# A hybrid layer on one core: instructions are recorded first and issued by a list scheduler written in the kernel

## Chip, core and metric

One core of a Trainium2 chip runs the whole kernel. The metric is device time in microseconds from the first to the last instruction of one execution. The times of the kernel before come from three runs. One further execution was taken with the hardware profiler, and all rows below are of that one.

## The reference

One layer of a trunk with five parallel head groups on 2048 tokens of width 1024, in float32. Cut to what matters:

```python
def hybrid_layer(x, mem, ...):
    h = rms_norm(x, norm_g)
    proj = h @ w_in                                  # one projection, 1024 -> 4652 columns
    pa, pb, pc, pd, pm = split_cols(proj, GROUP_COLS)
    ya = spatial_gating(...)                         # A: gMLP, chunks of 128 tokens
    yb = forgetting_attention(...)                   # B: FoX, causal attention with decay
    yc = mlstm(...)                                  # C: matrix memory, chunks of 128
    yd = rwkv7_time_mix(token_shift(pd, rwkv_mu), ...)   # D: delta rule, a state carried over all tokens
    ym = memory_attention(...)                       # M: attention to 256 memory tokens
    branches = [(ya, a_z), (yb, b_z), (yc, c_z), (yd, d_z), (ym, m_z)]
    mixed = jnp.concatenate([y * jax.nn.silu(z) for y, z in branches], axis=-1)
    return x + mixed @ w_out                         # 1280 -> 1024
```

Each group has 4 heads of width 64.

## The kernel before

**Stages.** Phase 1 normalises x, projects the columns of RWKV-7 (blocks `Dk`, `narrow`, `Dr`, `Dv`, `Dz`) for four quarters of 512 tokens, and runs RWKV-7 (`front` and `back`) beside it. Phase 2 goes over the quarters again for the columns of the mLSTM and of FoX, with the mLSTM beside it, and the RWKV-7 that is left. Phase 3 projects the columns of the gMLP and of the memory attention and runs FoX beside it. Then comes the output projection (line 878), with the memory attention beside its beginning. In the profiled execution phase 1 runs from 0 to about 245 us, phase 2 begins to mix with it there and goes on to about 960 us, phase 3 ends at about 1470 us, the memory attention at about 1602 us.

**Projections.** Weights come from DRAM into `wraw` (line 210, on SP's DMA queue), are split into two float32r parts `wt` by ACT (line 221) and DVE (line 224), and are multiplied with the two parts `ht` of the normalised tokens (ACT line 328, DVE line 329). The matmuls into the PSUM banks `pj` are lines 266, 277, 288, 300 and 314. They use the full 128*128 array. The norm of the tokens comes from `rstd`, which loads x a second time into `xt` (line 362, also on SP).

**Work beside them.** Most other matmuls have operands of 64 rows or 64 columns and take part of the array. In a profile's row the numbers before the tile's shape say which: 128*64 is all rows and half of the columns. In the attentions, line 1080 and line 1083 make scores in `p`, ACT takes the exponential to `pe` (line 1085), POOL adds these up (lines 1097, 1099), and line 1106 multiplies them with `v` into `acc`, in 64 columns of the array. RWKV-7's chain from chunk to chunk is line 1462 (`sv,gt`), a copy to `xc`, line 1471 (`xc,x`), a copy to `qv`, lines 1479 and 1481, and two DVE instructions that make the next `sv`. `front` computes 1/|k| of each token and head in `rn`: `rsqrt` (lines 151 to 155) does this by Newton's steps in eleven small DVE instructions, each of which reads what the one ahead of it wrote; line 1307 stands ahead of them, and PE's line 1319 waits for the last. In the attentions, `maxima` ends in line 1019, which makes `mm`, and PE's line 1067 waits for that.

**What sets the order.** `body` is Python that emits instructions. While it emits a projection it calls `tick()` after every few matmuls:

```python
    def tick():
        step_w()
        evac.tick()
        for l in lanes.values():
            l.tick()
```

`step_w` goes on with the loading of the next weights, `evac` holds what reads finished projections, and each lane is a queue of generators that goes on by its rate (`RATES`: gate 0.4, mlstm 0.8, front 1.0, back 1.33, fox 1.815 stages for each tick). So each engine's order is first the order of the program, with small pieces of the side work sprinkled between parts of the projections by fixed rates. The framework (Tile) then puts in the waits, assigns the buffers, and moves instructions by a cost model of its own.

Of the kernel before, what the change touches and what calls it, by code (L numbers as in the profile page):

```python
# [18 lines left out]
P = 128  # L19
# [16 lines left out]
# 256-column blocks of the input projection, by the first column of each  # L36
# [8 lines left out]
# narrow columns: (first column, width, first row of the transposed block)  # L45
NARROW = [(3340, 16, 0), (2564, 4, 16), (2568, 4, 20), (1536, 4, 24), (3868, 16, 32)]

# columns of the packed per-partition parameters
# [15 lines left out]
class Lane:  # L64
    """a queue of work that is emitted a stage at a time, between the parts of the projections"""
# [19 lines left out]
class Crowd:  # L85
    """short pieces of work that go on side by side, a stage at a time; a stage that has read a projection for the last
    time gives FREE"""
# [9 lines left out]
    def add(self, g, kind=None, most=2):  # L97
        """kind: what takes the same buffers, of which there are so many"""
        while sum(k == kind for _, k in self.all) >= most and kind:
            self.tick()  # L100
        if self.step(g):
            self.all.append((g, kind))
# [8 lines left out]
    def then(self, g):  # L111
        """g, behind all that is under way now"""
# [5 lines left out]

@with_exitstack
def body(ctx: ExitStack, tc, x, xT, mem, memT, wp, wkv, wout, pv, wa, sguT, sgub, out, dbg=None):  # L120
    nc = tc.nc
# [16 lines left out]
    ident = cp.tile([P, P], F32, name="ident")  # L138
    make_identity(nc, ident)
# [7 lines left out]
    def rsqrt(t):  # L147
        """in place, of up to 16 positive columns: half of the exponent, negated, then Newton's steps to the last bit"""
# [8 lines left out]
    # parameters that stand behind a tanh, a doubled SiLU or a doubled GELU  # L157
# [47 lines left out]
    def load_w(parts, src, ncol=256):  # L205
        """hi and lo parts of a block of 256 columns, 2 row blocks to a tile"""
# [42 lines left out]
    def W(n):  # L249
        """the weights of this block; those of the next one are sent for"""  # L250
# [9 lines left out]
    def proj_T(wt, m, hts):  # L260
        """[128 columns, 512 tokens] of the projection"""
# [10 lines left out]
    def proj_narrow(wt, hts):  # L272
        """64 columns: the products of their hi parts above those of the lo parts"""
# [8 lines left out]
    def proj_T2(wt, hts, then=None):  # L282
        """both halves of a block at once: for the last use of the row blocks"""
# [10 lines left out]
    def proj_tok2(wt, hts, then=None, ntile=4):  # L294
        """all tokens at once"""
# [11 lines left out]
    def proj_tok(wt, hts, i):  # L307
        """[128 tokens, 256 columns] of the projection, twice: tokens i * 128 on and the next 128"""
# [11 lines left out]
    def split_h(hts, src_of, g, N):  # L320
        """hi and lo parts of (normalised x) * g, one tile for each of the 8 row blocks"""
# [16 lines left out]
    def send(*a):  # L338
        """the next row blocks are sent for"""
        nxt[0] = []  # L340
        nxt[1] = split_h(nxt[0], *a)
        next(nxt[1])
        return nxt[1]
# [6 lines left out]
    def rstd(pool, tags, src, ntile):  # L350
        """1/rms of each token, tokens on partitions; tags: of the buffers for half of the columns of 128 tokens"""
# [20 lines left out]
    def rstd_rows(pool, tags, rb, src, ntile):  # L372
        """1/rms of each token, as a row over all partitions"""
# [4 lines left out]
    def over(ss, rb, ntile):  # L378
        """from tokens on partitions to a row over all partitions"""
# [5 lines left out]
    def gate(pt, o, then=lambda: None, free=FREE):  # L385
        """twice the SiLU"""
# [6 lines left out]
    def head_norm(pt, n, eps, pool=None):  # L393
        """1/rms over the 64 columns of each head; n columns on 128 tokens"""
# [13 lines left out]
    def qk_post(y, scale, d):  # L408
        """normalised over each head, scaled, transposed: to d"""
# [30 lines left out]
    def tok_cols(wt, hts, i, d):  # L440
        """tokens on partitions, to DRAM"""
# [10 lines left out]
    with ExitStack() as c1:  # L452
# [12 lines left out]
        def first(hts):  # L465
            """the first tokens: the norm is put to what comes out, so that the products need not wait for it"""
# [58 lines left out]
        for q in range(NQ):  # L525
# [8 lines left out]
            def shifted(pt, j, then):  # L534
                """token shift of a block of 128 columns"""
# [72 lines left out]
        evac.drain()  # L608

# [1142 lines left out]
```

## Time and profile before

| | us |
|---|---|
| three runs | 1751.72, 1748.99, 1744.91 |
| median | 1748.99 |
| span of the profiled execution | 1753.3 |
| PE busy | 1654.2 (94%), 11306 matmuls |
| DVE busy | 1197.5 (68%), 2990 instructions |
| ACT busy | 880.9 (50%), 1895 instructions |
| POOL busy | 302.8 (17%), 356 instructions |
| mean granted TensorE clock | 0.977 |

The profiled execution's own time is known by its span alone, which is 4.3 us over the median of the three runs. Busy times come from the page of the profile. Matmuls are pipelined and their ends are modelled, so a busy PE is not a PE at its peak: the time from the start of one group of matmuls to the start of the next tells more than the busy share.

### The profile page before, as it was taken

Reading aid. Unit: us, or ns where it says so; the run is one execution under the profiler, and the core shown is the slowest. Engines: PE = TensorE matmul, PEld = TensorE weight load, DVE = VectorE, ACT = ScalarE, POOL = GpSimd, SP = SyncE. Lnnn points to the kernel's source line nnn. Section 1 sums busy time; section 2 is a strip of 40 time slices with the busy share of each in tenths; the row PEclk is TensorE's granted clock in tenths of the full one; section 3 lists DMA queues with packets and bytes.
Section 4 is the critical chain, followed back from the end, with each engine's and each line's share of the span. In section 5 each row is a group of like instructions: output and inputs, shape, how many; then the busy total and the mean of one; then the engine's idle time right before and its main releaser. Section 6 shows DMA issues by size and latency. Waiting matters only on the chain.

```text
span 1753.3 us, 31654 instructions
## 1 busy us (share of the span) xinstructions
PE 1654.2 (94%) x11306; PEld 1282.0 (73%) x11306; DVE 1197.5 (68%) x2990; ACT 880.9 (50%) x1895; POOL 302.8 (17%) x356
## 2 busy tenths in 40 slices
PE   8889999899999999999999899998999998899999
PEld 6667777787978888787888666756655665577887
DVE  7688684775978579587766986878576777642220
ACT  5566654544464545446455765565555657531110
POOL 5020000010101001010000244354444142000000
PEclk9999999899999999999999999999999999899999
DMA  6878554443544354344435554434324335754431
GB/s 207 259 236 245 179 173 101 137 118 94 144 130 122 104 149 124 85 123 129 119 88 167 148 152 112 109 95 121 85 78 111 106 77 162 184 142 122 129 125 59
DMA packets 200151, 234.36 MB, mean 134 GB/s; under 512 B 75016, under 2 KB 107336, under 8 KB 199992
## 3 DMA queue, kind: packets, MB, share of 16 engines
q1 hardware_dynamic: 185144, 218.69, 43.6%
q10 hardware_dynamic: 14848, 13.64, 2.6%
q8 instruction: 89, 1.46, 0.4%
q14 instruction: 70, 0.57, 0.1%
HBM read 180.44 MB, written 51.81 MB: 132 GB/s over the span
## 4 chain that ended last, share of the span: by engine, by line
PE 58%; DVE 18%; DMA 14%; ACT 6%; issue 4%; SPq 1%; POOL 0%; ACTq 0%; DVEq 0%; POOLq 0%
PE pj L266 12%; PE pj L878 12%; PE pj L314 11%; DMA wraw<-in_wp 4%; PE pj L288 3%; PE acc L1106 3%; DMA xr<-hbd 3%; DVE wt L224 2%; PE wk L1025 2%; DMA ao<-dn 2%; PE p L1080 2%; PE p L1083 1%; PE pj L300 1%; DMA xr<-in_xT 1%; DVE rq L153 1%
## 5 line engine op out<-in xcount | busy, mean ns | idle before, releaser
L266 PE MATMUL pj<-ht,wt 128*128 128x512 f32 x1632 | 427.6, 404 | 6.0 <-ACT ht L328 4.2
L266 PEld LDWEIGHTS pj<-ht,wt 128*128 128x128 f32 x1632 | 298.3, 190 | 83.8 <-issue 9.8
L314 PE MATMUL pj<-wt,ht 128*128 128x256 f32 x2400 | 337.3, 292 | 6.9 <-ACT ht L328 2.4
L314 PEld LDWEIGHTS pj<-wt,ht 128*128 128x128 f32 x2400 | 308.1, 195 | 24.6 <-issue 5.8
L224 DVE TENSOR_TENSOR wt<-wraw,wt 128x512 fp32r<-128x512 f32 (+1 forms) x312 | 220.3, 709 | 94.0 <-ACT wt L221 92.5
L221 ACT CAST wt<-wraw 128x512 fp32r<-128x512 f32 (+1 forms) x312 | 184.7, 600 | 148.8 <-DMA wraw<-in_wp 103.1
L878 PE MATMUL pj<-wo,mt 128*128 128x512 f32 x960 | 232.7, 399 | 2.5 <-ACT wo L829 2.3
L878 PEld LDWEIGHTS pj<-wo,mt 128*128 128x128 f32 x960 | 180.3, 190 | 53.7 <-issue 6.9
L1099 POOL TENSOR_TENSOR es<-es,pe 128x512 f32<-128x512 f32 (+3 forms) x128 | 155.2, 1212 | 107.9 <-ACT pe L1085 99.2
L288 PE MATMUL pj<-ht,wt 128*128 128x512 f32 x480 | 135.5, 421 | 13.3 <-ACT wt L221 12.4
L1085 ACT ACTIVATE pe<-p 128x512 f32<-128x512 f32 x192 | 100.7, 541 | 67.9 <-PE p L1083 65.4
L1039 DVE TENSOR_REDUCE mx<-wk 128x1 f32<-128x512 f32 (+3 forms) x192 | 112.5, 615 | 16.6 <-PE wk L1025 11.2
L288 PEld LDWEIGHTS pj<-ht,wt 128*128 128x128 f32 x480 | 91.2, 199 | 38.1 <-ACT wt L221 12.8
L1106 PE MATMUL acc<-pe,v 128*64 128x512 f32 (+3 forms) x384 | 106.9, 580 | 5.9 <-DVE at L1139 5.1
L1097 POOL TENSOR_TENSOR es<-pe 128x512 f32<-128x512 f32 (+1 forms) x32 | 43.3, 1353 | 249.3 <-ACT pe L1085 207.1
L329 DVE SCALAR_TENSOR_TENSOR ht<-xr,pvt,ht 128x512 fp32r<-128x512 f32 (+1 forms) x88 | 68.6, 786 | 24.8 <-ACT ht L328 24.1
L858 ACT CAST mt<-mr 128x256 fp32r<-128x256 f32 x80 | 31.9, 406 | 102.7 <-DVE xr L882 45.9
L1080 PE MATMUL p<-qa,kb 128*128 128x512 f32 x192 | 76.9, 400 | 6.7 <-ACT pe L1085 6.7
L328 ACT ACTIVATE ht<-xr,pvt 128x512 fp32r<-128x512 f32 (+1 forms) x88 | 61.0, 701 | 42.5 <-DMA xr<-hbd 26.7
L882 DVE TENSOR_TENSOR xr<-pj,xr 128x512 f32<-128x512 f32 x32 | 22.0, 688 | 85.6 <-PE pj L878 85.5
L1025 PEld LDWEIGHTS wk<-ka,qb 66*128 66x128 f32 x224 | 40.4, 191 | 49.5 <-issue 17.7
L1025 PE MATMUL wk<-ka,qb 66*128 66x512 f32 (+3 forms) x224 | 72.5, 378 | 4.2 <-DVE mx L1039 1.4
(332 smaller groups left out, 2471.5 us busy)
## 6 DMA issues: line engine op xcount, KB each, us to landing
wraw<-in_wp SPq DMA_DIRECT2D x288, 256.0 KB
xr<-hbd SPq DMA_DIRECT2D x56, 256.0 KB
mr<-mix SPq DMA_DIRECT2D x80, 128.0 KB
xr<-in_x SPq DMA_DIRECT2D x32, 256.0 KB
out<-xr ACTq DMA_DIRECT2D x32, 256.0 KB
xt<-in_x SPq DMA_DIRECT2D x24, 256.0 KB
xr<-in_xT SPq DMA_DIRECT2D x24, 256.0 KB
hbd<-xr SPq DMA_DIRECT2D x24, 256.0 KB
```

The costliest lines, as they stand in the source:

```text
L221: A.copy(wt[:, :, 0, :ncol], raw[:, :, :ncol])
L224: V.tensor_tensor(lo, raw[:, :, :ncol], wt[:, :, 0, :ncol].bitcast(F32), op=ALU.subtract)
L266: T.matmul(pt, wt[k // 2][:, k % 2, a, m * P:(m + 1) * P], hts[k][:, b, :], start=n == 0, stop=n == 3 * KT - 1)
L288: T.matmul(pts[m], wt[k // 2][:, k % 2, a, m * P:(m + 1) * P], hts[k][:, b, :], start=k + n == 0, stop=k == KT - 1 and n == 2)
L314: T.matmul(pt[:, ii * 256:ii * 256 + 256], hts[k][:, a, (i + ii) * P:(i + ii + 1) * P], wt[k // 2][:, k % 2, b, :], start=n == 0, stop=n = ...
L878: T.matmul(po, mts[i // 2, k][:, a, i % 2 * P:(i % 2 + 1) * P], wo[e * NK + k][:, b], start=n == 0, stop=n == 3 * NK - 1)
L1025: T.matmul(p1, self.qb[0:66, i * P:(i + 1) * P], self.k[kk][0][0:66, :w], start=True, stop=True, skip_group_check=diag)
L1039: V.tensor_reduce(*late.pop(), axis=AX.X, op=ALU.max)
L1080: T.matmul(p2[:, f:], kb[:, ks], self.qa[:, f:], start=True, stop=False)
L1085: A.activation(e[:, f:], p2[:, f:], AF.Exp)
L1099: G.tensor_tensor(self.sum[:, f:], self.sum[:, f:], e[:, f:], op=ALU.add)
L1106: self.att.nc.tensor.matmul(self.acc[64 * i:64 * i + 64, f:], self.v[:, kt], e[:, f:], start=kt < 2, stop=True, skip_group_check=True)
```

## The change

`body` now runs with `nc = rec = Recorder(tc.nc, tc)` and with the framework's own re-ordering switched off. A call such as `V.tensor_tensor(...)` no longer issues anything. It is kept as an `Op` with the operations that it depends on (found from the boxes of the tiles that it reads and writes) and a price in nanoseconds. At five places `rec.flush()` issues all that was recorded since the last one: at the end of phase 1, between phases 2 and 3 (where the pools change), at the end of phase 3, behind the last unit of the attentions, and at the end of the program. No instruction moves across a flush. Rates, stages, tiles, buffers and the instructions themselves stay as they were, and comments are taken out. The diff, cut to its core:

```diff
+    def price(self, o):
+        if o.fn == "dma_start":
...
+            o.cost, o.lag, o.key = 400.0, 1900.0, packets * each / 16
+        if e == "tensor":
...
+            q = [32 if x <= 32 else 64 if x <= 64 else 128 for x in (rows, cols)]
+            if lhs.dtype == F32R:
+                c = max(n / 2.4 + 14, 60.0)
...
+            o.cost, o.mode, o.lag = c, tuple(q), 200.0
...
+        if e == "vector":
+            if o.fn in ("tensor_tensor", "scalar_tensor_tensor", "tensor_reduce"):
+                o.cost = 150 + 1.06 * n
...
+    SWITCH = {True: 95.0, False: 100.0}
+
+    def flush(self):
...
+        while left:
+            best = None
+            for e, lst in cand.items():
+                if not lst:
+                    continue
+                c = self.pick(e, lst, first)
+                if c and (best is None or c[:2] < best[:2]):
+                    best = c
+            start, _, o = best
+            cand[o.eng].remove(o)
+            self.place(o, start, live)
...
+        for o in order:
+            getattr(getattr(self.nc, o.eng), o.fn)(*o.a, **o.k)
...
+    def after(self, p, o):
+        if p.eng == o.eng and p.fn != "dma_start":
+            return 0.0
+        return p.done + self.SEM
...
+    def pick(self, e, lst, first):
...
+            s = max(clk, o.ready, r + self.SEM if r else 0.0)
+            n = o.n
+            if e == "tensor" and self.mode not in (None, FULL):
+                if o.mode != FULL and o.mode == self.mode and s <= clk + 60:
+                    n -= 1 << 30
+                elif o.mode != FULL and s <= clk + 60:
+                    n -= 1 << 29
+            c = (s, n, o)
...
-    nc = tc.nc
+    nc = rec = Recorder(tc.nc, tc)
+    ctx.enter_context(tc.manual_schedule())
...
+        rec.flush()
```

In words: of all operations whose predecessors are placed, the one that can start first by these prices is placed next. Of those that can start together, the one that comes first in the program goes first. PE has one more rule: while the array is in a part shape, a matmul of the same shape that can start within 60 ns goes ahead of all others, and then one of any part shape. An operation on the same engine as its predecessor costs no lag (`after`). Buffers of a tag are given out in the order of the program (`room`).

The instructions are the same in number on each engine; their order differs. Three places show how. (All rows of the kernel after carry line 350, where `flush` issues them, so tiles tell what they are.)

PE, FoX beside the projections of phase 3, where `p` are score banks with the program's running numbers. Before:

```order
L314 MATMUL pj<-wt,ht 128x256 x12
L1080 MATMUL p_16855<-qa,kb 128x512
L1083 MATMUL p_16855<-qb,ka 128x512
L1106 MATMUL acc<-pe,v 64x512 x2
L1080 MATMUL p_16866<-qa,kb 128x512
L1083 MATMUL p_16866<-qb,ka 128x512
L314 MATMUL pj<-wt,ht 128x256 x12
L1080 MATMUL p_16888<-qa,kb 128x512
L1083 MATMUL p_16888<-qb,ka 128x512
L1106 MATMUL acc<-pe,v 64x512 x2
L1080 MATMUL p_16896<-qa,kb 128x512
```

After:

```order
L350 MATMUL p_12971<-qa,kb 128x512
L350 MATMUL p_12971<-qb,ka 128x512
L350 MATMUL p_12973<-qa,kb 128x512
L350 MATMUL p_12973<-qb,ka 128x512
L350 MATMUL wk<-ka,qb 128x256 x2
L350 MATMUL pj<-wt,ht 128x256 x8
L350 MATMUL acc<-pe,v 64x512 x8
L350 MATMUL pj<-wt,ht 128x256 x4
L350 MATMUL p_12978<-qa,kb 128x512
```

Four to eight `acc<-pe,v` matmuls now stand in one row where two stood, with fewer returns to the projections `pj` between. Over the whole program, PE comes back from a part shape to the full array 268 times, where it was 365 (phase 1 44 and 44, phase 2 169 and now 141, phase 3 134 and now 74, output projection 17 and now 9). Changes from one part shape to another are 121, where they were 106.

DVE, the inverse norm `rn` of RWKV-7's `front`, from its first to its last instruction (before, only the first half of it). Before:

```order
L1307 TENSOR_SCALAR rn<-wk 128x8
L1404 TENSOR_TENSOR xs<-xs,xtmp 128x3x23
L151 TENSOR_SCALAR rq<-rn 128x8
L1309 SCALAR_TENSOR_TENSOR ag<-th,gi 128x512
L1403 TENSOR_TENSOR xtmp<-xs,at 128x3x22
L153 TENSOR_TENSOR rq<-rq 128x8
L1311 TENSOR_SCALAR th<-th,hp_70 128x256
L1404 TENSOR_TENSOR xs<-xs,xtmp 128x3x22
L154 SCALAR_TENSOR_TENSOR rq<-rq,rn 128x8
L1311 TENSOR_SCALAR th<-th,hp_70 128x256
L1403 TENSOR_TENSOR xtmp<-xs,at 128x3x21
L155 SCALAR_TENSOR_TENSOR rq<-rq 128x8
```

After:

```order
L350 TENSOR_SCALAR rn<-wk 128x8
L350 TENSOR_SCALAR rq<-rn 128x8
L350 TENSOR_TENSOR rq<-rq 128x8
L350 SCALAR_TENSOR_TENSOR rq<-rq,rn 128x8
L350 SCALAR_TENSOR_TENSOR rq<-rq 128x8
L350 TENSOR_TENSOR rq<-rq 128x8
L350 SCALAR_TENSOR_TENSOR rq<-rq,rn 128x8
L350 SCALAR_TENSOR_TENSOR rq<-rq 128x8
L350 TENSOR_TENSOR rq<-rq 128x8
L350 SCALAR_TENSOR_TENSOR rq<-rq,rn 128x8
L350 SCALAR_TENSOR_TENSOR rn<-rq 128x8
L350 SCALAR_TENSOR_TENSOR ag<-th,gi 128x512
```

The eleven instructions stand one behind the other now. Before, 15 to 28 rows lay between the first and the last in the eight blocks; nine of them are its own. Over the program, 1428 of DVE's instructions read what the one directly ahead of them wrote; before, 653 did.

SP's DMA queue in phase 1, where `xt` are the second loads of x for the norm and `wraw` the weights (of `Dz`, here). Before:

```order
L582 DMA gated<-sh 12x512
L362 DMA xt<-in_x 128x512 x3
L584 DMA smd<-sh 16x2x512
L362 DMA xt<-in_x 128x512 x3
L584 DMA smd<-sh 16x2x512
L362 DMA xt<-in_x 128x512 x2
L553 DMA d_r<-sh 128x512
L210 DMA wraw<-in_wp 128x512 x3
```

After:

```order
L350 DMA xt<-in_x 128x512
L350 DMA hbd<-x_137 128x512
L350 DMA wraw<-in_wp 128x512
L350 DMA xr<-in_xT 128x512
L350 DMA gated<-sh 12x512
L350 DMA smd<-sh 16x2x512 x2
L350 DMA hbd<-x_145 128x512
L350 DMA wraw<-in_wp 128x512
L350 DMA d_r<-sh 128x512
L350 DMA xt<-in_x 128x512
L350 DMA wraw<-in_wp 128x512
L350 DMA xt<-in_x 128x512
```

Before, all eight loads of `xt` stand ahead of the first weights of `Dz`; now the weights stand between the loads of `xt`, the first of them behind one.

At the flush between phases 1 and 2 no projection stands between three steps of RWKV-7's chain on PE: `rw<-sv,gt`, `rw<-xc`, `rw<-qv,gt` and the next `rw<-sv,gt` follow each other directly.

## Rows read from the trace of the kernel before

**Rows 1.** Span of the core and its mean granted TensorE clock.

```profile
core 0: 1753.3 us, clock 0.977
```

**Rows 2.** Windows: length, busy PE, PEld, DVE, ACT, POOL, clock, DMA share, GB/s.

```profile
360.00:960.00 600.00, 584.89 (x5435) 497.00 (x5436) 438.11 (x1359) 297.92 (x662) 40.97 (x89) 0.99 0.42 121
960.00:1470.00 510.00, 478.95 (x2639) 330.17 (x2637) 386.20 (x740) 302.06 (x597) 196.62 (x161) 0.97 0.42 112
...
1602.00:1753.30 151.30, 147.56 (x641) 119.26 (x633) 33.26 (x65) 16.34 (x41) 0.00 (x0) 1.00 0.34 107
sum 1753.30, PE 1654.17 PEld 1282.02 DVE 1197.49 ACT 880.86 POOL 302.84; mean PE 275.70 PEld 213.67 DVE 199.58 ACT 146.81 POOL 50.47
```

**Rows 3.** The page's chain that ended last: share of the span by engine.

```profile
PE 58%; DVE 18%; DMA 14%; ACT 6%; issue 4%; SPq 1%; POOL 0%; ACTq 0%; DVEq 0%; POOLq 0%
```

**Rows 4.** The chain, 250 to 350 us: start, length, undisturbed projections with their count.

```profile
260.99 10.88 PE pj L288 x48
271.87 5.99 PE pj L314 x50
```

**Rows 5.** PE's timeline, 286 to 289 us, RWKV-7: start, length, line, tiles, array, count.

```profile
286.02 0.45 PE L1462 MATMUL rw<-sv,gt 128*64 128x64 f32 x8
286.40 0.75 PE L314 MATMUL pj<-wt,ht 128*128 128x256 f32 x4
287.08 0.48 PE L1471 MATMUL rw<-xc,x 64*64 64x64 f32 x8
...
288.15 0.69 PE L1479 MATMUL rw<-qv,gt 128*64 128x64 f32 x16
288.77 0.33 PE L1481 MATMUL rw<-sv,rk 64*64 64x64 f32 x2
```

**Rows 6.** PE's timeline, 1444 to 1446 us, FoX beside a projection.

```profile
1444.19 1.66 PE L266 MATMUL pj<-ht,wt 128*128 128x512 f32 x6
1445.78 0.65 PE L1106 MATMUL acc<-pe,v 128*64 128x256 f32 x4
```

**Rows 7.** PE's waits by releaser: us in total, times, longest us.

```profile
PE pj L288 <- ACT wt L221: 12.4, 2, 7.5
PE wk L1067 <- DVE mm L1019: 11.5, 8, 3.1
PE wk L1319 <- DVE rn L155: 8.6, 6, 3.0
...
PE acc L1106 <- DVE at L1139: 5.1, 3, 2.5
...
PE wk L1146 <- DVE mx L1039: 4.1, 2, 3.7
```

**Rows 8.** DVE's timeline, 237 to 248 us: first and last instruction of one `rn`.

```profile
237.79 0.16 DVE L1307 TENSOR_SCALAR rn<-wk 128x8 f32<-128x8 f32 x1
...
247.78 0.15 DVE L155 SCALAR_TENSOR_TENSOR rn<-rq 128x8 f32<-128x8 f32 x1
```

**Rows 9.** DVE's timeline, 21 to 24 us: neighbours, the first two independent, the last dependent.

```profile
21.77 0.16 DVE L151 TENSOR_SCALAR rq<-ss 128x4 int32<-128x4 int32 x1
21.84 0.28 DVE L224 TENSOR_TENSOR wt<-wraw,wt 128x128 fp32r<-128x128 f32 x1
...
23.39 0.15 DVE L154 SCALAR_TENSOR_TENSOR rq<-rq,ss 128x4 f32<-128x4 f32 x1
23.58 0.16 DVE L155 SCALAR_TENSOR_TENSOR rq<-rq 128x4 f32<-128x4 f32 x1
```

**Rows 10.** SP's timeline, 41 to 52 us: first `xt` loads, and the weights behind all.

```profile
41.28 1.60 SPq L362 DMA_DIRECT2D xt<-in_x  x3
...
51.56 1.45 SPq L210 DMA_DIRECT2D wraw<-in_wp  x3
```

**Rows 11.** Windows around PE's gap in phase 1; columns as in rows 2.

```profile
53.20:58.20 5.00, 0.05 (x2) 0.01 (x1) 1.18 (x8) 1.64 (x7) 0.00 (x0) 0.79 0.84 266
56.10:62.90 6.80, 4.71 (x15) 3.80 (x16) 4.67 (x16) 3.09 (x5) 0.00 (x0) 0.50 0.76 249
```

More of the change, by code (lines that the diff above doesn't have):

```diff
@@ L138, in body @@
     ident = cp.tile([P, P], F32, name="ident")
-    make_identity(nc, ident)
+    make_identity(tc.nc, ident)
     pvt = cp.tile([P, NPV], F32, name="pvt")
@@ L772, in body @@
                     l.step()
+            rec.flush()
             csp.close()
@@ L815, in body @@
     evac.drain()
+    rec.flush()
     cw.close()
@@ L839, in body @@
         fox.step()
+    rec.flush()
     att.c5.close()
@@ L884, in body @@
                 nc.scalar.dma_start(out[r, es], xr)
+    rec.flush()
     att.close()
```

238 lines of the change are left out of this document (added).

## The prediction

> **What bounds the kernel now.** I began with the span and the clock [rows 1], then the windows by stage [rows 2], then the chain that ended last [rows 3]. PE is busy for 1654.2 of 1753.3 us and idle for 99.1 (the difference in the sum row). DVE, the next, has 438 of 600 us in phase 2 and 386 of 510 in phase 3. PE holds 58% of the chain and DVE 18%. So PE sets the time, and two kinds of loss can be looked for on it: time in which it is busy but slower than it could be, and time in which it waits.
>
> *Busy but slow.* Undisturbed projections set the scale: 48 matmuls of 512 columns in 10.88 us, 0.2267 each, and 50 of 256 columns in 5.99 us, 0.1198 each [rows 4]. Beside RWKV-7 four of the latter take 0.68 us from their start to the start of what follows (286.40 to 287.08), where 4 x 0.1198 = 0.48 would do: 0.20 us go when PE returns from a part of the array to the whole [rows 5]. On the way in, eight `sv,gt` matmuls take 0.38 us (286.02 to 286.40), while sixteen like them take 0.62 (288.15 to 288.77). Eight more cost 0.24, so the first eight carry 0.14 of their own. A round trip costs 0.20 + 0.14 = 0.34 us. FoX's products show the same: six projections take 1.59 us (1444.19 to 1445.78) where 6 x 0.2267 = 1.36 would do, 0.23 on the way out [rows 6]. At 365 trips this is about 124 us of PE's busy time.
>
> *Waiting.* The longest waits are for weights (ACT `wt`, 12.4 us) and for ends of DVE's chains: `mm` 11.5, `rn` 8.6, `at` 5.1, `mx` 4.1, together 29.3 [rows 7]. The largest single gap is in phase 1: PE has 0.05 us of work in 53.2 to 58.2, and the clock granted behind it, from 56.1 to 62.9, is 0.50 of full speed, 1.2 GHz instead of 2.4 [rows 11]. The mean clock of 0.977 [rows 1] says what such stretches take over the whole: 0.023 x 1753 = 40 us, if PE had work in all of them.
>
> **The change part by part.** Its instructions are the same, so it can only remove losses or add some.
>
> *A, round trips.* The order after has 97 returns to the whole array fewer, 60 of them in phase 3 and 28 in phase 2, and 15 more changes from one part shape to another. 97 x 0.34 = 33.0 us less. A change between part shapes has no row of its own; I put it at the entry's 0.14, so 15 x 0.14 = 2.1 us more. A gives -31. All of it lies on PE, which has least slack: in 360 to 960 us it is busy for 584.9 of 600 [rows 2]. The other bound is 0, where the time saved on PE comes back as waiting.
>
> *B, weights ahead of the second loads of x.* All eight `xt` loads stand in SP's queue ahead of the weights of `Dz`, from 41.28 to 51.56 us [rows 10], and the gap of 4.95 us follows. After, only one stands ahead. The `xt` loads that weights now pass are late instead; what waits for them is the norm of the first tokens, on ACT and DVE, whose product comes behind the matmuls. I count the gap, -5.0, and leave the 3.4 us that the half clock takes of the next 6.8 (half of them) for the bound: 0 to -8.4. The DMA engines are busy for 0.76 to 0.84 of that time [rows 11], so transfers are not made faster by being re-ordered.
>
> *C, PE's other waits.* Of the 99.1 us idle, 5.0 are in B and 3.7 in the last stage (151.30 less 147.56), which has no side work to move: some 90 are left. The `rn` chain now lasts from 237.79 to 247.78, 10.0 us, with up to 19 other instructions in it [rows 8]. With eleven neighbours at 0.195 us each (23.39 to 23.58) [rows 9] it takes 2.1, so its 8.6 us of waits go. Between the first and the last of `mm` the order has 2.2 rows where it had 3.7 on the mean: 1.5 rows less of at most 0.7 us, for 8 waits, -7. Together -16. Of the rest, 90 - 16 = 74, the scheduler's order takes the shorter ones by time and not by fixed rates. Nothing in the trace prices that; between none and half (-37) I take a fifth, -15, since most of them end with an engine that itself has little slack. With a third of the idle time gone (31 of 90) a third of the 40 us of low clock could go, -13; short waits carry less of it, so I take -10. C gives -41, bounds 0 and -80.
>
> *D, flushes.* Nothing moves across a flush. At the one between phases 1 and 2, three steps of RWKV-7's chain now stand with no projection between. A step takes 1.06 us (286.02 to 287.08), 0.38 of it matmuls [rows 5], so 0.68 lie open: 3 x 0.68 = 2. Two such flushes, 4 us; the others fall where only one kind of work is left. Bounds 0 and +10 (five flushes).
>
> *E, dependent neighbours on DVE.* An instruction that reads what the one ahead of it wrote starts 0.195 us after it; an independent one starts 0.07 after it (21.77 to 21.84) [rows 9]. So each new pair costs DVE 0.12 us, and there are 1428 - 653 = 775 more: 93 us on DVE, from 1197 to about 1290. DVE has idle time to hide this (162 us in 360 to 960, 124 in 960 to 1470 [rows 2]). Where the cover is gone the cost is one for one. I take DVE's share of the chain, 18% [rows 3]: +17, bounds 0 and +93.
>
> [...]
>
> *Sum.* -31 - 5 - 41 + 4 + 17 = -56. Against the profiled execution's span this is 1753.3 - 56 = 1697. That span lies 4.3 us over the median of the three runs, 1749.0, so the time to forecast is 1749 - 56 = **1693 us**. With half of A and of C it would be 1729; with E at nothing, 1676.
>
> **The rivals.** *1, more of the waits go.* If half of the 90 us of waits and half of the 40 us of clock go, with A at -33, B at -8.4, D at +4 and E at 0, the sum is -45 - 20 - 33 - 8 + 4 = -102: 1647 us. For it: every engine but PE has about a third of its time free or more, and the order is made with all engines in view. Against it: the scheduler's prices are fixed figures, and its lag on the same engine is zero, which rows 9 contradict.
>
> *2, what feeds PE sets the pace.* PE's savings come back as waits, since the projections cannot go on before ACT and DVE have read the banks and delivered `ht` and `wt`. A is 0, C halves to -20: -5 - 20 + 4 + 17 = -4, 1745 us, no change. For it: 42% of the chain is not PE [rows 3], and DVE has only 24% free in phase 3. Against it: in phase 2 PE idles for 15 us of 600 only, and nothing that feeds it is near 100%.
>
> The Trainium skill, "TensorEngine Tiling (Array Packing)", section "PSUM Bottleneck", says that using parts of the array speeds up TensorE but not the reading of PSUM, which may then become the bottleneck. Here fewer trips squeeze the same reads into less time; by that rule rival 2 is the outcome, while the 68% of DVE and 50% of ACT speak for room.
>
> *3, slower: DVE becomes what PE waits for.* DVE takes its queue in order, so a chain of eleven dependent instructions, 2.1 us, now holds up every weight split and bank copy behind it, where before these stood in its gaps. If that keeps all of C's waits in place and 62 of the 93 us (two thirds) reach PE, the sum is -31 - 5 + 4 + 62 = +30: 1779 us. It decides from the point where, with C at 0, 41 of the 93 us (44%) land on PE: -31 - 5 + 4 + 41 = +9. For it: 29.3 us of waits already end with DVE [rows 7]. Against it: DVE's 286 us of idle time in phases 2 and 3, and the chains end sooner for those who wait for them.
>
> That the change does not do what it says is ruled out by the order: the counts in A are the kernel's own.
>
> **How the numbers follow.** Chances: forecast 0.50 (its own range 1670 to 1720), rival 1 0.22, rival 2 0.13, rival 3 0.15. About 0.5% (8.7 us) is what a measurement of this kernel can tell from no change. Forecast and rival 1 are faster, with a part of rival 2: 0.75. Same is most of rival 2, 0.11. Slower is rival 3 with its nearer part, 0.14. The range goes from 1635 (a little beyond rival 1) to 1755 (rival 2, and the point at which rival 3 begins), which leaves out most of rival 3 and the ends of rival 1.
>
> **What would show it.** A: `acc` rows of six to eight in phase 3, and PE's time from the start of a product to the next projection unchanged, 0.20 to 0.23 over the steady rate. B: no PE gap around 53 us, weights of `Dz` on the way before 45 us. C: PE's waits for `rn` near 0 and for `mm` under 5 us, idle time near 65 us, mean clock over 0.98. D: three short gaps where phase 1 ends. E: DVE busy or bound in short gaps for about 90 us more, with the eleven `rn` instructions 0.19 to 0.20 apart. The forecast is wrong if PE's idle time stays near 99 us or grows (rivals 2 and 3; in 3 most of its waits end with DVE), or if DVE's pairs cost PE more than 31 us. It is also wrong if a trip does not cost 0.34 us when eight matmuls stand in a row instead of two.

## The result: 1.3% slower, and where PE's time went

The kernel after takes 1774.05 us (median of 4 runs, 1769.09 to 1778.78), the kernel before 1748.8 (4 runs). The ratio is 1.0129, with a 95% interval from 1.0095 to 1.0164: some 23 us slower, where the forecast was 56 us faster. Since the kernel before was run again beside each group of experiments, what follows compares ratios to it; 0.01 is 17.5 us.

The page of the kernel after: span, busy times, and the chain by engine; then span and clock.

```profile
span 1769.2 us, 31645 instructions
...
PE 1638.6 (93%) x11306; PEld 1293.1 (73%) x11306; DVE 1263.1 (71%) x2990; ACT 882.3 (50%) x1895; POOL 305.0 (17%) x356
...
PE 47%; DVE 22%; DMA 19%; issue 4%; ACT 4%; SPq 1%; ACTq 1%; POOL 0%; DVEq 0%; POOLq 0%
```

```profile
core 0: 1769.2 us, clock 0.971
```

PE is busy for 15.6 us less than before (1654.2) and idle for 1769.2 - 1638.6 = 130.6 us, 31.5 more than the 99.1 of [rows 2]. DVE is busy for 65.6 us more. In the chain PE falls from 58% to 47%, DVE goes from 18 to 22 and DMA from 14 to 19 [rows 3]. The mean clock falls from 0.977 [rows 1] to 0.971: 0.029 x 1769 = 51 us at most, where it was 40.

To compare stages, the windows are cut in each kernel where the projections of phases 1, 2 and 3 end. Columns as in [rows 2]. Before:

```profile
0.00:271.90 271.90, 245.11 (x1379) 189.44 (x1380) 203.37 (x507) 158.68 (x373) 39.85 (x74) 0.97 0.69 211
271.90:952.30 680.40, 656.15 (x6013) 555.21 (x6011) 496.17 (x1526) 341.52 (x758) 51.20 (x110) 0.98 0.42 120
952.30:1477.50 525.20, 491.78 (x2726) 340.65 (x2725) 393.11 (x755) 309.33 (x612) 197.73 (x162) 0.97 0.43 115
1477.50:1753.30 275.80, 261.14 (x1193) 196.72 (x1191) 104.84 (x203) 71.32 (x156) 14.07 (x11) 0.98 0.44 127
```

After:

```profile
0.00:293.50 293.50, 257.74 (x1555) 195.32 (x1557) 214.75 (x511) 160.25 (x383) 35.64 (x73) 0.95 0.61 191
293.50:987.40 693.90, 648.26 (x5837) 556.76 (x5837) 533.30 (x1520) 335.41 (x735) 52.59 (x108) 0.97 0.42 118
987.40:1486.40 499.00, 469.65 (x2725) 344.23 (x2724) 408.52 (x749) 311.27 (x612) 203.92 (x165) 0.99 0.41 115
1486.40:1769.20 282.80, 262.99 (x1192) 196.79 (x1192) 106.55 (x210) 75.39 (x167) 12.88 (x10) 0.96 0.47 137
```

Phase 3 is 26.2 us shorter (525.2 to 499.0): 60 of the 97 saved returns are there, and its clock is higher as well (0.99 where it was 0.97). Phase 1 is 21.6 longer, of which a part is RWKV-7's work done earlier (1555 matmuls where there were 1379). Phase 2 has 176 matmuls and 7.9 us of PE's work less, and is 13.5 us longer all the same, so PE is idle for 45.6 us there instead of 24.3. DVE has 37 us more to do in it. The last stage is 7.0 longer. Together these make the 15.9 us between the two spans.

PE's waits in the kernel after (us in total, times, longest):

```profile
PE pj L350 <- DVE wt L350: 17.7, 17, 3.9
PE pj L350 <- ACT wt L350: 16.5, 7, 7.6
PE p L350 <- ACT pe L350: 12.1, 10, 4.7
PE pj L350 <- DVE ht L350: 8.4, 7, 2.9
...
PE wk L350 <- DVE mm L350: 3.9, 9, 1.1
...
PE wk L350 <- DVE rn L350: 0.9, 2, 0.6
```

The waits that the prediction named have shrunk: `rn` from 8.6 to 0.9, `mm` from 11.5 to 3.9 [rows 7]. Others have grown, for weights above all. Projections now wait 17.7 us for DVE's half of them and 16.5 for ACT's, which was 13.5 before. For DVE's half, the two largest waits of the kernel before were these:

```profile
PE pj L277 <- DVE wt L224: 1.7, 1, 1.7
...
PE pj L314 <- DVE wt L224: 0.7, 2, 0.3
```

One such place, in rows of the kernel after. ACT's timeline first: it has copied a block of weights by 680.51 (679.89 + 0.62), and the split that DVE has to make of it may begin then.

```profile
679.89 0.62 ACT L350 CAST wt<-wraw 128x512 fp32r<-128x512 f32 x1
```

DVE's timeline, from just ahead of that:

```profile
679.83 0.17 DVE L350 TENSOR_SCALAR rq<-rs 128x8 int32<-128x8 int32 x1
680.04 0.17 DVE L350 TENSOR_TENSOR rq<-rq 128x8 f32<-128x8 f32 x1
...
682.64 0.17 DVE L350 TENSOR_SCALAR rq<-rs 128x8 int32<-128x8 int32 x1
...
687.40 0.69 DVE L350 TENSOR_TENSOR wt<-wraw,wt 128x512 fp32r<-128x512 f32 x1
```

And PE's:

```profile
688.14 2.08 PE L350 MATMUL pj<-wt,ht 128*128 128x256 f32 x8 [3.93 <-DVE wt L350]
```

An `rsqrt` that has just begun, a second one behind it, and other work, of RWKV-7 above all, stand ahead of the split. An `rsqrt` has ten instructions; with the one that feeds it that makes the chain of eleven of the prediction, at 0.20 us from start to start, each reading what the one ahead of it wrote. The split of the weights waits for 6.9 us in DVE's queue (680.51 to 687.40), and PE for 3.93.

A second kind of place, beside the output weights `wo`. ACT's timeline:

```profile
1500.80 0.62 ACT L350 CAST wo<-wr 128x512 fp32r<-128x512 f32 x1 [1.89 <-issue]
...
1503.43 0.62 ACT L350 CAST wo<-wr 128x512 fp32r<-128x512 f32 x1 [1.20 <-DMA wr<-in_wout]
1504.43 0.62 ACT L350 CAST qa<-kr 128x512 fp32r<-128x512 f32 x1 [0.38 <-DMA kr<-qk_Mq]
1504.96 0.59 ACT L350 ACTIVATE pe<-p 128x512 f32<-128x512 f32 x1
```

PE's at the same time:

```profile
1500.94 0.63 PE L350 MATMUL p<-qa,kb 128*128 128x512 f32 x1
1505.60 0.80 PE L350 MATMUL p<-qa,kb 128*128 128x512 f32 x1 [4.03 <-ACT pe L350]
```

The scores that `pe` reads are there by about 1501.6 (1500.94 + 0.63). But ACT stands before copies whose loads have not landed (it waits for them for 1.20 and 0.38 us more), with the exponential queued behind them, and PE waits for 4.03 us. In the scheduler's account a load takes 0.4 us to issue and lands 1.9 us plus its transfer later, about 3 us for 256 KB. Of the 17 weight loads of 256 KB in the chain of the kernel after, 15 take 3.6 to 6.9 us and two take 2.7 and 2.9. The chain has the loads that were waited for, so the mean of all may be lower. Two of them:

```profile
41.01 4.04 DMA wraw<-in_wp
...
435.85 6.94 DMA wraw<-in_wp
```

### The profile page after: what moved, and what is told of

Its sections match the earlier page's. It is cut to its first block, busy times and chain, and to the rows that moved or that the text cites. A ratio compares the mean times of both kernels' runs of the same rounds, so it can differ in the third digit from the quotient of the medians.

```text
span 1769.2 us, 31645 instructions
## 1 busy us (share of the span) xinstructions
PE 1638.6 (93%) x11306; PEld 1293.1 (73%) x11306; DVE 1263.1 (71%) x2990; ACT 882.3 (50%) x1895; POOL 305.0 (17%) x356
## 3 DMA queue, kind: packets, MB, share of 16 engines
q8 instruction: 89, 1.46, 0.4%
## 4 chain that ended last, share of the span: by engine, by line
PE 47%; DVE 22%; DMA 19%; issue 4%; ACT 4%; SPq 1%; ACTq 1%; POOL 0%; DVEq 0%; POOLq 0%
PE pj L350 32%; PE rw L350 6%; PE wk L350 5%; DMA wraw<-in_wp 4%; DVE wt L350 3%; DVE rq L350 3%; PE p L350 2%; PE acc L350 2%; DMA xr<-in_xT 2%; DVE xtmp L350 2%; DMA xr<-hbd 2%; DVE xs L350 2%; DMA mr<-mix 1%; DVE mx L350 1%; SPq L350 1%
## 5 line engine op out<-in xcount | busy, mean ns | idle before, releaser
L350 PE MATMUL pj<-ht,wt 128*128 128x512 f32 x2176 | 576.4, 409 | 32.6 <-ACT wt L350 9.7
L350 PEld LDWEIGHTS pj<-ht,wt 128*128 128x128 f32 x2176 | 405.1, 193 | 140.6 <-DVE wt L350 15.4
L350 PE MATMUL pj<-wt,ht 128*128 128x256 f32 x2784 | 396.3, 293 | 19.3 <-DVE wt L350 9.3
L350 PEld LDWEIGHTS pj<-wt,ht 128*128 128x128 f32 x2784 | 359.5, 195 | 40.3 <-DVE wt L350 10.9
L350 DVE TENSOR_TENSOR wt<-wraw,wt 128x512 fp32r<-128x512 f32 (+1 forms) x312 | 232.3, 750 | 79.0 <-ACT wt L350 78.4
L350 POOL TENSOR_TENSOR es<-es,pe 128x512 f32<-128x512 f32 (+3 forms) x128 | 159.8, 1249 | 97.0 <-ACT pe L350 91.0
L350 PE MATMUL acc<-pe,v 128*64 128x512 f32 (+3 forms) x384 | 100.1, 569 | 8.2 <-ACT pe L350 5.6
L350 ACT ACTIVATE ht<-xr,pvt 128x512 fp32r<-128x512 f32 (+1 forms) x88 | 60.8, 701 | 55.3 <-DMA xr<-hbd 31.5
L350 PE MATMUL p<-qb,ka 68*128 68x512 f32 x192 | 74.7, 392 | 0.0
L350 DVE TENSOR_TENSOR xtmp<-xs,at 128x60 f32<-128x60 f32 (+24 forms) x248 | 61.2, 247 | 6.5 <-DMA at<-ad 2.6
L350 PEld LDWEIGHTS acc<-pe,v 128*64 128x64 f32 x384 | 28.0, 137 | 50.8 <-issue 24.7
```

The costliest lines, as they stand in the source:

```text
L350: getattr(getattr(self.nc, o.eng), o.fn)(*o.a, **o.k)
```

## The experiments

Two theories stood after this. **D**: DVE's dependent neighbours cost it some 90 us (step E of the prediction) and hold up what PE needs. **M**: loads are priced too short, so engines stand blocked before work whose data is on its way.

The expectations count dependent neighbours by the operations themselves: 534 before, 1220 after. The counts of 653 and 1428 in the change go by the tiles' names without buffer numbers, and so take in neighbours that work on different buffers.

**Each price alone.** The first edit charges a DVE instruction by the rows and lets one that reads its neighbour's output start only 114 ns later, so that other work is put between. The second lets a DMA land later.

```diff
-            return 0.0
+            if p.eng == "vector" and p.outs & o.ins:
+                return p.done + 84.0        # done is the end plus 30
+            return 0.0
...
+            o.cost -= 80                    # e == "vector"
```

> The kernel after with one price changed: a DVE instruction is priced 80 ns less, and one that reads what the instruction ahead of it on DVE wrote may start 114 ns after that one's end at the earliest (rows 9 give both). The scheduler then puts other work between: by the order, neighbours that depend on each other fall from 1220 rows to 612 (before: 534), and PE's returns to the whole array stay at 265 (after: 268). Theory D, dependent neighbours on DVE cost the time: DVE's busy time falls from 1263 to about 1205, PE's waits for the weights (wt, 34 us of waits by DVE and ACT) about halve, PE's idle time falls from 131 to about 100 us, and the time from 1774 to about 1735 (1720 to 1750). Theory M, loads are priced too short, so engines stand blocked behind them: 1765 to 1778, PE's waits as they are.

```diff
-            o.cost, o.lag, o.key = 400.0, 1900.0, packets * each / 16
+            o.cost, o.lag, o.key = 400.0, 3200.0, packets * each / 16
```

> The kernel after with one price changed: a DMA lands 3.2 us after its issue plus its transfer, not 1.9 (in the chain of after, loads of 256 KB take 4.0 to 4.9 us, where the old price gives about 3). Neighbours on DVE that depend on each other stay (1224 rows), PE's returns are 284 (after: 268). Theory M, loads priced too short: ACT waits less for wraw (148 us of idle time ended by it in after, 103 before), PE's idle time falls by 15 to 25 us, the time to 1745 to 1758. Theory D: 1768 to 1782, with 16 more returns worth 5 us more.

Measured: 1756.07 us for the first, ratio 1.0042 [1.0015, 1.0069]; 1752.98 for the second, ratio 1.0000 [0.9973, 1.0026]. Both gain on the after's 1.0129. The second is as M expected. The first lies between the two expectations: DVE's busy time and PE's waits for weights (`wt`, 34.2 us after, 13.5 here) fall as D said, and the time gains less than half of what D said. The page's row of the first, with DVE back near the 1197.5 of before:

```profile
PE 1630.0 (93%) x11306; PEld 1289.5 (74%) x11306; DVE 1207.4 (69%) x2990; ACT 882.2 (50%) x1895; POOL 307.3 (18%) x356
```

In the second, ACT waits less for weights. ACT's waits for them, before and after:

```profile
ACT wt L221 <- DMA wraw<-in_wp: 103.1, 66, 7.0
```

```profile
ACT wt L350 <- DMA wraw<-in_wp: 148.5, 95, 6.6
```

Second experiment, and the first:

```profile
ACT wt L350 <- DMA wraw<-in_wp: 77.8, 54, 7.8
```

```profile
ACT wt L352 <- DMA wraw<-in_wp: 92.4, 69, 5.8
```

So this wait falls with either price, and it is down to 107.6 us also in the slowest kernel of all (DVE's price lowered alone, below). What shows that the price of loads counts is the time of the second experiment, not this row.

**Both prices together.**

The two edits above in one kernel.

> Both prices of the two kernels above together; dependent neighbours 606, returns 267. Theory D alone: as the first, about 1735. Theory M alone: as the second, 1745 to 1758. Both: the gains add, 1710 to 1725.

1721.49 us, ratio 0.9826 [0.9786, 0.9866]: 1.7% faster than the kernel before. On the kernel after that is 0.0303, 53 us, where the two alone gave 15 and 23; that it is more than their sum is barely clear of the noise. Its page:

```profile
span 1720.3 us, 31692 instructions
...
PE 1626.4 (95%) x11306; PEld 1289.9 (75%) x11306; DVE 1205.8 (70%) x2990; ACT 877.8 (51%) x1895; POOL 307.7 (18%) x356
```

Its waits of PE and of ACT:

```profile
PE pj L352 <- DVE wt L352: 5.2, 6, 2.3
```

```profile
ACT wt L352 <- DMA wraw<-in_wp: 50.0, 43, 3.8
```

PE is idle for 1720.3 - 1626.4 = 93.9 us instead of 130.6, and its waits for DVE's half of the weights fall from 17.7 to 5.2.

A second dose of the price of loads, on the kernel with both:

```diff
-            o.cost, o.lag, o.key = 400.0, 3200.0, packets * each / 16
+            o.cost, o.lag, o.key = 400.0, 4500.0, packets * each / 16
```

> The fourth experiment with a DMA landing 4.5 us after its issue plus its transfer, not 3.2: a second dose. Dependent neighbours 643, returns 282. If loads at 3.2 were still priced too short (the chain of after has 4.0 to 4.9 us with the transfer, which 3.2 + 0.75 meets): 1712 to 1718. If 3.2 meets them: 1718 to 1732, the 15 returns more costing 2 to 5 us.

1719.80 us, ratio 0.9804 [0.9770, 0.9838]: as expected if 3.2 us meets the loads. The second dose can't be told from the first.

**Is it scatter between orders?** Three controls change a price that should mean nothing, the scheduler's time from engine to engine.

```diff
-    SEM = 70.0
+    SEM = 80.0
```

> A control for all of the others: the kernel after with the scheduler's time from one engine to another at 80 ns instead of 70, a change that should mean nothing. The order changes in detail; dependent neighbours on DVE 1222 (1220), PE's returns 273 (268). If orders that differ by chance scatter little, 1768 to 1782 (after 1774, 1.013 of before), and the gains of 16 to 21 us of the first two experiments are theirs. If they scatter by 15 us or more, one of these controls falls outside.

The same at 60 ns:

> The same with 60 ns; dependent neighbours 1223, returns 273. 1768 to 1782 if orders scatter little.

And 80 ns on the kernel with both prices:

> The fourth experiment (both prices, 1721, 0.983 of before) with 80 ns instead of 70; dependent neighbours 608, returns 282. 1715 to 1730 if orders scatter little and both prices are what gains.

1776.72, ratio 1.0173 [1.0134, 1.0211]; 1777.75, ratio 1.0165 [1.0127, 1.0203]; and with both prices 1722.90, ratio 0.9859 [0.9820, 0.9898]. All three are as expected, and orders of the same kind lie within 0.006 of each other, some 10 us. The kernel after and its two controls average 1.0156; the kernels with both prices (fourth, seventh and this one) 0.9830. The two prices are worth 0.033, some 57 us, well over that scatter; alone, against 1.0156, the DVE price is worth 20 and the DMA price 27.

**Is it the pairs or their price?** The first edit changed two things. Its first half alone:

```diff
+            o.cost -= 80                    # e == "vector", nothing in after()
```

> Control for the first experiment: the kernel after with DVE instructions priced 80 ns less, but no price on neighbours that depend on each other. By the order these stay (1286 rows; 1220 after, 612 in the first experiment); PE's returns are 256. Theory D (it is the dependent neighbours): no gain, 1765 to 1785, DVE busy about 1260. Rival (it is DVE's price that was too high, and any order made with lower ones is better): 1750 to 1760, as the first experiment.

1840.92 us, ratio 1.0499 [1.0461, 1.0537], far outside of both expectations. The page:

```profile
span 1842.8 us, 31713 instructions
...
PE 1663.8 (90%) x11306; PEld 1311.3 (71%) x11306; DVE 1252.6 (68%) x2990; ACT 883.3 (48%) x1895; POOL 302.5 (16%) x356
```

DVE is about as busy as in the kernel after (1252.6 where it was 1263.1), and PE is idle for 179 us. So the pairs' own time is not all: the price itself, when it is too low for 1286 pairs, costs another 0.037, 65 us. That the scheduler then lines the others up for results that come later is the likely way, and is not shown. The old price of 150 ns and more was too high for an independent instruction (0.07 us to the next start [rows 9]) and too low for a dependent one (0.195), and these errors may have balanced in the kernel after, which was not tried by itself. So I formed a new theory, that the price and not the pairs was the loss, and charged the pairs truly without any gain from parting them:

```diff
+        if e == "vector":
+            if self.prev is not None and self.prev.outs & o.ins:
+                cost += 114
+            self.prev = o
         self.clk[e] = start + cost
```

> The kernel after with DVE priced as the rows show it (80 ns less, and 114 ns more where an instruction reads what the one just ahead of it wrote), but the 114 ns are charged as time in which DVE is taken, so that nothing is gained by putting other work between. The scheduler knows the cost of its own order now and still makes it: dependent neighbours 1218 (after 1220; 612 in the first experiment), PE's returns 276. If the 93 us of DVE's own time are what the change loses (theory D as the prediction had it): 1766 to 1782, DVE busy about 1260. If it is the wrong price, by which other engines are lined up for results that come later, and not the time itself: 1750 to 1760, as in the first experiment, though DVE stays as busy.

With the edit of the second experiment beside it:

> The same with a DMA landing 3.2 us after its issue plus its transfer (as in the second and fourth experiments: 1753 and 1721). Dependent neighbours 1238, returns 283. If DVE's own time is what counts: 1748 to 1756, no better than the second. If the price is what counts: 1720 to 1728, like the fourth.

1785.36 us, ratio 1.0175 [1.0131, 1.0220], and 1756.29, ratio 1.0022 [0.9993, 1.0050]: both within 4 us of the upper end of what was expected if the pairs' own time counts. Against the fifth experiment, which has the same lower price and no charge for pairs, the charge gains 1.0499 - 1.0175 = 0.0324, 57 us: that much a price costs that is too low for the pairs. But as an account of the kernel after the new theory falls: a scheduler that knows what its pairs cost but keeps them gains nothing on the kernel after (1.0129) or on the second experiment (1.0000). Against kernels with equal prices for the rest, parting the pairs gives 1.0175 - 1.0042 = 0.0133, 23 us, and with the DMA price 1.0022 - 0.9826 = 0.0196, 34 us. Each is good to some 9 us (0.005). The orders with the pairs parted have 606 and 632 of them fewer, some 75 to 80 us of DVE's time at 0.125 (0.195 - 0.07 [rows 9]), so a third to two fifths of it reaches the end. They also have 11 and 16 returns to the whole array fewer, worth 1 to 3 us by the next experiments.

**What are the round trips worth?** PE's rule for part shapes is left out, once on the kernel after and once with both prices.

```diff
-            if e == "tensor" and self.mode not in (None, FULL):
-                if o.mode != FULL and o.mode == self.mode and s <= clk + 60:
-                    n -= 1 << 30
-                elif o.mode != FULL and s <= clk + 60:
-                    n -= 1 << 29
```

> The kernel after without PE's rule that prefers matmuls of the same part shape. By the order, returns to the whole array go from 268 to 374 and all changes of shape from 657 to 872 (before: 365 and 836); DVE's order stays as dependent as it was (1235 rows). If a round trip costs 0.34 us of time that counts: 106 x 0.34 = 36 us more, 1800 to 1815. If what PE saves comes back as waiting (the prediction's second rival): 1770 to 1780, with PE's idle time down by some 30 us.

> Both prices corrected (the fourth experiment, 1721), without PE's rule for matmuls of the same part shape: returns to the whole array 368, with the rule 267; dependent neighbours 652. On the kernel after the rule was worth 14 us only, for 106 returns. If that was so because PE stood waiting for DVE and loads, each return costs more here, where PE waits less: 25 to 35 us, 1746 to 1756. If a return that counts is simply worth 0.14 us: 1733 to 1738.

1788.35, ratio 1.0206 [1.0163, 1.0249], and 1742.21, ratio 0.9932 [0.9906, 0.9959]. Both lie between their two expectations, the sixth nearer the lower one. The pages, third experiment first:

```profile
span 1788.8 us, 31661 instructions
...
PE 1673.1 (94%) x11306; PEld 1292.6 (72%) x11306; DVE 1259.4 (70%) x2990; ACT 882.9 (49%) x1895; POOL 304.1 (17%) x356
```

```profile
span 1740.3 us, 31678 instructions
...
PE 1653.2 (95%) x11306; PEld 1285.4 (74%) x11306; DVE 1213.5 (70%) x2990; ACT 879.8 (51%) x1895; POOL 304.8 (18%) x356
```

On the kernel after, 106 returns more cost PE 1673.1 - 1638.6 = 34.5 us of busy time, 0.33 each. But its idle time falls from 130.6 to 115.7, so 14.9 of the 34.5 were only waiting in another form; the time moves by 0.0077, 13 us. With both prices 101 returns cost 26.8 us of busy time, 0.27 each, 6.8 come back, and the time moves by 0.0106, 19 us. Both differences in time are good to some 9 us, so they don't show whether a return counts for more where PE waits less. The mean clock tells the two busy times apart: it is 0.967 in the third experiment and 0.971 after, up to 0.004 x 1789 = 7 us of the 34.5, but 0.974 and 0.973 in the sixth and the fourth. So 0.27 is the better figure for a trip.

**Two more prices that the rows correct.**

```diff
-            o.cost = (165 if ps else 205) + 0.835 * n
+            o.cost = (75 if ps else 115) + 0.835 * n
```

> The fourth experiment (1721) with ACT's instructions priced 90 ns less as well: in the trace of after the next ACT instruction starts 0.09 us before the end of the one ahead (706.49 + 0.63 against 707.03). Dependent neighbours on DVE 611, returns 252 (267 in the fourth). If a price that is nearer the rows pays whichever engine it is: 1705 to 1716. If ACT, idle for half of the time, takes no part in what PE waits for: 1716 to 1726, of which 15 returns fewer would give 2 to 3.

```diff
-    SWITCH = {True: 95.0, False: 100.0}
+    SWITCH = {True: 200.0, False: 140.0}
...
-                if o.mode != FULL and o.mode == self.mode and s <= clk + 60:
+                if o.mode != FULL and o.mode == self.mode and s <= clk + 300:
...
-                elif o.mode != FULL and s <= clk + 60:
+                elif o.mode != FULL and s <= clk + 300:
```

> The fourth experiment (1721) with a change of array shape priced at 200 ns back to the whole array and 140 ns to a part (rows 5: 0.20 and 0.14; in the change 95 and 100), and the rule that prefers part shapes reaching 300 ns ahead instead of 60. Returns 261 (267), all changes 637 (652), so PE's order gains 6 returns, 1 to 2 us. If only the counts matter: 1717 to 1724. If PE's model, now slower by some 38 us over the program (267 x 145 ns), is what the others were lined up wrongly for: 1705 to 1715.

1730.15, ratio 0.9831 [0.9802, 0.9861], and 1733.95, ratio 0.9860 [0.9824, 0.9897] (the kernel before took 1760.4 beside them): neither is told from the fourth experiment. So a price nearer the rows did not pay as such for ACT or for PE's shapes.

Not tried: the kernel without flushes (pools are closed behind them), and the order of before with only the framework's own re-ordering switched off, which is a part of the change.

## The prediction, step by step

**What bounds the kernel** was read rightly: PE sets the time, and losses are trips and waits.

**A, round trips, was right in kind and too large twice.** The order does what it counts. But a trip costs PE some 0.27 us (sixth experiment), where 0.34 was taken. The return's 0.20 holds: the projections that stand undisturbed between matmuls of part shapes take 0.21 us over the steady rate before (median of 163 groups) and 0.19 after (119 groups; 0.20 behind six or more part-shape matmuls in a row). By these figures it is the entry's 0.14, read from one place, that was too high. PE's busy time fell by 15.6 us and not by 31; up to 11 of the rest is the lower clock (0.977 to 0.971). The second fault is that the sum put all 31 us on the end. By the third and sixth experiments 0.13 to 0.18 us of each return count, so 97 of them are worth 12 to 18 us. The rest comes back as PE waiting, which is the second rival, true in part. The sentence that failed is "all of it lies on PE, which has least slack".

**B failed.** The gap behind the `xt` loads is gone, and the bound that the prediction named beside it (the norm of the first tokens is late instead) came true in full. PE's timeline of the kernel after:

```profile
65.52 2.08 PE L350 MATMUL wk<-ident,ss 128*128 128x128 f32 x8 [5.61 <-DVE ss L350]
```

4.95 us of waiting for weights became 5.61 of waiting for the norm; in 52 to 62 us the DMA engines are busy for 0.97 of the time. By these rows it is worth 0, not -5; no run takes B by itself.

**C is the step that failed most.** Its named parts held: `rn` and `mm` wait 15.3 us less (7.7 and 7.6), where 16 was taken. But the sum then let a fifth of the other waits go, and a quarter of the low clock, for no row at all, only because the order is made with all engines in view. In fact the scheduler orders by an account of time of its own, and where a price in it is wrong the order is worse by as much as the experiments show. All waits and gaps together rose by 31.5 us, and the low clock behind them by up to 11, where -41 was summed. The DMA price of 1.9 us was in the diff, and the chain of before had 16 weight loads of 256 KB, at 2.8 to 10.2 us, 14 of them over 3.1; one of them, and a load of x:

```profile
42.00 3.16 DMA xt<-in_x
...
51.56 5.88 DMA wraw<-in_wp
```

The prediction weighed the prices as a remark against its first rival and gave them no term. The second experiment measures that term at 23 to 27 us (against the kernel after, and against its mean with the controls). Beside a DVE price nearer the rows it is 27 (1.0175 - 1.0022 = 0.0153) and 38 (1.0042 - 0.9826 = 0.0216).

**D held.** At the flush between phases 1 and 2 the chain stands open three times. PE's timeline:

```profile
294.71 0.73 PE L350 MATMUL rw<-xc,x 64*64 64x64 f32 x8 [0.86 <-ACT xc L350]
296.31 0.87 PE L350 MATMUL rw<-qv,gt 128*64 128x64 f32 x16 [0.87 <-ACT qv L350]
...
299.23 0.70 PE L350 MATMUL rw<-sv,gt 128*64 128x64 f32 x8 [1.45 <-DVE sv L350]
```

0.86 + 0.87 + 1.45 = 3.2 us, where 2 was taken for one flush. At the one between phases 2 and 3 PE waits for 1.46 us (at 988.87, for DVE's `gz`), so the two come to about 5, where 4 was summed.

**E had nearly the right size on DVE and was small on the end.** DVE's busy time rose by 65.6 us. The dependent instruction also starts some 34 ns after its neighbour's end, where an independent one starts 80 ns before it. The 775 pairs were too many: by the operations themselves it is 686 (1220 - 534), 86 us at 0.125, where 93 was taken. In the traces, 510 neighbours before and 1225 after, of those that share a tile's name, start that late: 715 more, 65.6 + 715 x 0.034 = 90. Of this 23 to 34 reach the end (eighth and ninth experiments, each against its fellow with the pairs parted), where 18%, +17, was taken from DVE's share of the chain. The third rival's mechanism is what the rows at 680 to 688 us show. Its price was put too high (62 us), and it does not bring the result alone: with the DMA price corrected and the pairs kept the kernel is even with the kernel before (1.0022). Its sign, that most of PE's waits end with DVE, did not come either: 58 of 125 us do (52 of 93 before), and 53 end with ACT (39 before). So it is luck that its 1779 us lies so near the measured 1774: it has A in full, 62 us for the pairs, and loads at nothing.

**The sum afterwards.** A -15, B 0, D +5, E +28, loads +27 make +45, against a measured +23. The remaining -22 is near C's named -16; it is a remainder and was not measured by itself. Against the forecast's -56, the largest misses are the loads, which had no term (27), and the 25 us (15 of waits, 10 of clock) that C let go for no row; then A (16), E (11) and B (5). Together that is 5 us more than the miss of 79. The range began to exclude the truth at 1755, since the third rival had to bring the slower side alone.

## To carry to other kernels

A scheduler that places work by prices is as good as the prices that decide who stands first in a queue that cannot be overtaken: look up each of them in the trace of before, above all for dependent neighbours and for loads, and give a wrong one a term of its own. Then ask of each saving on the bounding engine how much comes back as its waiting; here a quarter to two fifths did (6.8 of 26.8 us, 14.9 of 34.5). If such a kernel is slower than it should be, one run for each price tells more than any view, and two prices together gave 1.7% on the kernel before.

## What the runs showed of the chip

In the rows at 679 to 688 us DVE's dependent instructions of 128 x 8 elements start 0.20 us after each other, 0.17 busy and the rest a gap. By the neighbours of [rows 9] an independent one starts 0.07 us after one of 128 x 4 elements.

That a price 80 ns too low for 1286 such pairs should cost 65 us of 1774, with no more work on any engine but 25 us on PE, was not expected. Part of it goes with the clock: its mean over the run fell to 0.949.

```profile
core 0: 1842.8 us, clock 0.949
```

0.051 x 1843 = 94 us at most, where the kernel after has 51. A gap on PE can cost twice, once for itself and once for the half clock (1.2 instead of 2.4 GHz) in which the work behind it begins. Before, 0.50 of the clock was granted from 56.1 to 62.9 us, while PE was waiting for 4.95 us and when it went on [rows 11]. In the kernel after it is 0.56 on the mean behind the wait of 5.61 us that ended at 65.52:

```profile
65.40:70.00 4.60, 4.48 (x16) 3.93 (x17) 2.57 (x6) 2.21 (x6) 0.00 (x0) 0.56 0.89 242
```
